# Neighbourhood scores: the low part of the queries in a zero-padded tile per head

## The chip, the cores and the metric

The kernel runs on one core of a Trainium2 chip. The metric is the time of one execution on the device in microseconds, lower is better. Engines are named as in the profile: PE is TensorE (PEld its weight load), DVE is VectorE, ACT is ScalarE, POOL is GpSimd, SP issues the DMAs.

## The reference

Two layers of a mixer work on 1024 latent tokens (a grid of 16 rows by 64 columns) and, as a prefix, 256 context tokens, 1024 features wide. In each layer one projection of the modulated input feeds three head groups: a gated convolution, a bidirectional retention (6 heads of 64) and a neighbourhood attention (6 heads of 64). The change is in the attention alone:

```python
s_loc = einsum('bhcd,bhrckd->bhcrk', q_r, k_win) * scale + bias   # window of 8 rows x 16 columns
s_ctx = einsum('bhcd,bhjd->bhcj', q_r, k_ctx) * scale             # all 256 context keys
p = softmax(concatenate([s_loc, s_ctx]))
o = p_loc @ v_win + p_ctx @ v_ctx
```

In the first layer the context tokens too are queries, over the context keys alone; the second layer needs no outputs for them.

## The kernel before

Everything is float32 in value. Matmuls whose result must be exact to float32 take their operands in two parts, a high one rounded to the matmul's fast format (`R`, float32r) and a low one that holds the rest (`x - high`). A product of two such operands is summed in three passes: high by high, low by high, high by low. Projections (`accumulate`, tile ps_pj) do so with three matmuls per 128 rows of contraction, over 512 or 256 columns.

For the scores a head has only 64 features, so two passes are packed into one matmul of 128 rows. For a pair of heads p, the key tile `KS[128, 2, TOK]` has for head hh the high part of its keys in rows 64*hh to 64*hh+63 and the low part in the other 64 rows. The query tile `QH[128, 2, TOK]` has the high part of the queries in both halves. `QH` by `KS` over 128 rows is thus high by high plus high by low. The missing low by high is a second matmul into the same bank, with `QL[128, TOK]`, which holds the low part of head 0's queries in rows 0 to 63 and of head 1's in rows 64 to 127. That matmul takes 64 rows: those of the head.

`natten_conv` runs once per layer. Keys and queries of a pair of heads are projected (`keys`, `queries`, with the evacuations `k_evac` and `q_evac`), then `core` runs as a side stream: it works through items, one step each, while the projections of the convolution, the gates and the next pair run between them. A latent item is a tile of 128 queries of one head (`s_lat`): scores over the 256 context keys (bank sc) and over a window of 384 keys, or 256 at the grid's two edges (bank sl), both from the ring ps_s of two banks; then on DVE the bias is added and the maximum taken (L746, L749, L751), ACT takes the exponential (L753), and DVE normalizes (L693, L694), all in the tile `P`. Two steps later (LAG = 2) `turn` transposes P on PE into ps_pt, and ACT and DVE copy it to `PT`. Two steps after that, for every second item, `pv` multiplies with the values of both heads (ps_pv). In a step the order on PE is: scores, then pv, then the transposes. A context item (`s_ctx`, layer 0 only, four per pair) has one score product over 256 keys.

The bias tables `B` (L713, L718) are built by POOL at the start of each pair. POOL also takes every fourth of the weight splits (L217) and some gate products (L364).

What sets the order: the program of PE stands in the order in which the code issues it. `Order` keeps a planned time `t`, to which every matmul adds its `cost`, and continues a side stream when its planned time has come. The other engines take their instructions in the order of the code's dependencies, and a tile ring (`bufs`) makes a writer wait for the buffer's last reader. `mm` is at L85 and `transpose` at L126, so all matmuls carry these two lines; they are told apart by tile names.

Of the kernel before, what the change touches and what calls it, by code (L numbers as in the profile page):

```python
# [30 lines left out]
LAG = 2  # L31
# [4 lines left out]


class Order:
    """Interleaves the matmul streams: the running one and those that wait for other engines."""

    def __init__(self):
        self.t = 0.0
# [36 lines left out]
def backbone(ctx: ExitStack, tc: tile.TileContext, io):  # L79
# [47 lines left out]
        od.t += 109  # L127
        od.poll()

    # ------------------------------------------------------- modulation tables  # L130
    class Mod:
        def __init__(self, l):
            self.l = l
# [2 lines left out]
            self.tab = const.tile([128, 24, 2], F, tag="mods", bufs=2, name="mods")  # L136

        def load(self, alloc, c0, w):
            """Two tiles [128, 4, w] of w_mod's columns c0:c0+w."""
            out = []  # L140
            for hf in range(2):
                t = alloc()
                sp.dma_start(t, io["w_mod"][self.l, hf * 512:(hf + 1) * 512, c0:c0 + w]
                             .rearrange("(k p) c -> p k c", p=128))
                out.append(t)
            return out
# [4 lines left out]
                   hf == 0, hf == 1, 80 * w // 128)  # L151

        def columns(self, ps, bank, parts):
            """Sums of the four row groups of ps, turned into columns of the table."""
            n = sum(k for _, k, _ in parts)
            m2 = const.tile([128, 512], F, tag="m2", name="m2")
            act.copy(m2[:, :n * 128], ps)
            yield 800
            pt = bank()
            for s in range(n):  # L160
                transpose(pt[:, s * 128:(s + 1) * 128], m2[:, s * 128:(s + 1) * 128])
            for o, k, blk in parts:
                t = const.tile([128, 4, 2], F, tag="msum", bufs=2, name="msum")
                dve.tensor_reduce(
                    t[:, :k], pt[:, o * 128:(o + k) * 128].rearrange(
                        "p (s g v) -> p s v g", g=4, v=32)[:, :, 0:2], AX.X, ALU.add)
                self.add_bias(t[:, :k], k, blk)
# [5 lines left out]
                ALU.add, ALU.add)  # L173

        def background(self, blocks, tmp):
            """The table's columns of some pairs of blocks, off the tensor engine."""
            def load(blk, kk):
                t = tmp.tile([128, 256], F, tag="wm", bufs=4, name="wm")
                sp.dma_start(t, io["w_mod"][self.l, kk * 128:(kk + 1) * 128,
                                            blk * 128:blk * 128 + 256])  # L180
                return t

            todo = [(blk, kk) for blk in blocks for kk in range(KC)]
            tiles = [load(*x) for x in todo[:2]]
            yield 2500
            for i, (blk, kk) in enumerate(todo):
                if i + 2 < len(todo):
                    tiles.append(load(*todo[i + 2]))
                t = tiles.pop(0)
                if kk == 0:  # L190
                    acc = const.tile([128, 2, 256], F, tag="m2", name="acc")
                for v in range(2):
                    c = cs[:, kk, v:v + 1]
                    if kk == 0:
                        dve.tensor_scalar(acc[:, v], t, c, None, ALU.mult)
                    else:
                        dve.scalar_tensor_tensor(acc[:, v], t, c, acc[:, v], ALU.mult, ALU.add)  # L197
                yield 2100
                if kk == KC - 1:
                    yield 1000  # L200
                    pt = ps_t()
                    for j in range(2):
                        for v in range(2):
                            o = (2 * j + v) * 128
                            transpose(pt[:, o:o + 128], acc[:, v, j * 128:(j + 1) * 128])
                    m = const.tile([128, 2, 2], F, tag="msum", bufs=2, name="msum")
                    dve.tensor_reduce(m, pt.rearrange("p (s v i) -> p s v i", s=2, v=2),
                                      AX.X, ALU.add)
                    self.add_bias(m, 2, blk)

    # ---------------------------------------------------------------- weights
    flip = [0]

    def split_lo(lo, raw, hi):
# [34 lines left out]
            t.append(split(raw, "w"))  # L249
        return lambda kk, i: t[kk // 2][i][:, (kk % 2) * 256:(kk % 2 + 1) * 256]  # L250

    # ------------------------------------------------------------------ input
    def new_h():
        return [[hpool.tile([128, KC, n], R, tag=f"h{j}{g}", name=f"h{j}{g}")
                 for j in range(2)] + [[]] for g, (o, n) in enumerate(GRP)]
# [24 lines left out]
                evac(g, ps[:, :GRP[g][1]], GRP[g][1])  # L280

    def h_tile(h, mods, t, xz, tmp):
        """Transposed, modulated and split columns of a token tile, as a side stream."""
        g = 2 if t >= 8 else t // 4
        off = t * 128 - GRP[g][0]
        v = 1 if g == 2 else 0
# [14 lines left out]
            pool.tensor_tensor(lo, ht, f32(hi), ALU.subtract)  # L301
            yield 1000

    # ---------------------------------------------------------------- decays
    def decay_tables(l, tmp):
        x = tmp.tile([128, 12], F, tag="dk", bufs=8, name="dk")
        sp.dma_start(x, io["decay"][l:l + 1, :].to_broadcast([128, 12]))
# [57 lines left out]
            sp.dma_start(yT[y_block * 128:(y_block + 1) * 128, o:o + n], y[:, :n])  # L365
        return f

    # ------------------------------------------------------------- retention
    def rope_evac(t2, rc, rs, dst, scale):
        def f(g, ps, n):  # L370
            o = GRP[g][0]
# [11 lines left out]
    def retention(l, h, yT, vn, ctx_q, begin):  # L383
        groups = (0, 1, 2)
        qgroups = groups if ctx_q else (0, 1)
        with ExitStack() as st:
# [33 lines left out]
            def core(p, kT, qT, V, oT):  # L420
# [29 lines left out]
                               kfb[:, hh].rearrange("p f d -> p (f d)"), True, True, 141)  # L450

                def chains():
                    """States before each chunk, transposed, in both directions."""
                    seqs = ([8, 9, 0, 1, 2, 3, 4, 5, 6, 7], [9, 8, 7, 6, 5, 4, 3, 2, 1, 0])
                    for fb in range(2):
                        dve.memset(ST[:, seqs[fb][0], fb], 0.0)
                    for i in range(9):
                        for fb in range(2):
                            a, b = seqs[fb][i:i + 2]
                            dve.scalar_tensor_tensor(  # L460
                                ST[:, b, fb], ST[:, a, fb], dec["gc"][:, fb, p:p + 1],
                                U(a)[:, fb * HD:(fb + 1) * HD], ALU.mult, ALU.add)
# [157 lines left out]
                proj_T(l, C_RG + 128 * p, gate_evac(t2, normed, Y_RET[p], yT),  # L620
                       h, (2, 0, 1) if ctx_q else (0, 1))

    # ------------------------------------------- neighbourhood and convolution
    def natten_conv(l, h, yT, vn, ctx_q, aside, w_out):
        qgroups = (2, 0, 1) if ctx_q else (0, 1)
        groups = (0, 1, 2) if ctx_q else (0, 1)
# [1 line left out]
        with ExitStack() as st:  # L628
# [3 lines left out]
            np_ = np_cm.__enter__()  # L632

            def flipped(t, o, rows):
                """Rows, blocks and columns of four tiles of reversed queries."""
                return bass.AP(tensor=t.tensor, offset=t[:, o:o + 1].offset,
                               ap=[list(t.ap[0]), [-8, rows], [8 * rows, 4], [-1, 8]])

# [19 lines left out]
            def q_evac(QH, QL):  # L658
                def f(g, ps, n):
# [14 lines left out]
                    for hh in range(2):  # L674
                        a, b = 64 * hh, 64 - 64 * hh
                        dve.tensor_copy(sel(QH[a:a + 64, hh]), src[a:a + 64])
                        act.copy(sel(QH[b:b + 64, hh]), src[a:a + 64])
                        dve.tensor_tensor(sel(QL[a:a + 64]), src[a:a + 64],
                                          f32(sel(QH[a:a + 64, hh])), ALU.subtract)
                return f  # L680

            def scores(dst, QH, QL, KS, hh, qo, ko, n):
                a = 64 * hh
                mm(dst, QH[:, hh, qo:qo + 128], KS[:, hh, ko:ko + n], True, False, n / 2.35)
                mm(dst, QL[a:a + 64, qo:qo + 128], KS[a:a + 64, hh, ko:ko + n], False, True,
                   n / 2.35)

            def col(nm):
                return np_.tile([128, 1], F, tag=nm, bufs=3, name=nm)
# [4 lines left out]
                dve.tensor_scalar(P[:, :n], P[:, :n], r, 0.5, ALU.mult, ALU.mult)  # L694

            def window(k):
                """First tile and number of tiles of the keys near a block of eight columns."""
                return max(k - 1, 0), 3 if 0 < k < 7 else 2

            def core(p, QH, QL, KS, oN):  # L700
# [22 lines left out]
                def s_ctx(i):  # L723
# [3 lines left out]
                    nm = col("nm")  # L727
                    dve.tensor_reduce(nm, sc[:, :256], AX.X, ALU.max)
                    dve.tensor_scalar(nm, nm, -1.0, None, ALU.mult)
                    P = np_.tile([128, 640], F, tag="P", bufs=LAG + 2, name="P")  # L730
                    s1 = col("sa")
                    act.activation(P[:, :256], sc[:, :256], AF.Exp, bias=nm, accum_out=s1)
                    normalize(P, 256, s1)
# [2 lines left out]
                def s_lat(i):  # L736
# [5 lines left out]
                    scores(sc[:, :256], QH, QL, KS, hh, k * 128, SEQ, 256)  # L742
                    scores(sl[:, :n], QH, QL, KS, hh, k * 128, k0 * 128, n)
                    m0, mx, nm = col("m0"), col("mx"), col("nm")
                    P = np_.tile([128, 640], F, tag="P", bufs=LAG + 2, name="P")
                    dve.tensor_tensor_reduce(  # L746
                        P[:, :256], sc[:, :256], zero.to_broadcast([128, 256]), 1.0, LOW,
                        ALU.add, ALU.max, m0)
# [6 lines left out]
                    return P  # L755

                def turn(P, nt):
                    PT = np_.tile([128, 640], F, tag="PT", bufs=4, name="PT")
                    pt = ps_t()
                    for i in range(min(nt, 4)):  # L760
                        transpose(pt[:, i * 128:(i + 1) * 128], P[:, i * 128:(i + 1) * 128])
# [94 lines left out]
                    yield from conv(b)  # L856

            cu = conv_units()
            KSs = [np_.tile([128, 2, TOK], R, tag="KS", name="KS") for _ in range(3)]
            state = {}  # L860

# [2 lines left out]

            def queries(p):
                QH = np_.tile([128, 2, TOK], R, tag="QH", bufs=1, name="QH")
                QL = np_.tile([128, TOK], R, tag="QL", bufs=1, name="QL")
                proj_T(l, C_NQ + 128 * p, q_evac(QH, QL), h, qgroups)
                return QH, QL

# [37 lines left out]
            next(cu)  # L908
            od.finish(job)

    # -------------------------------------------------------------- layers
    mod = Mod(0)
    h = new_h()
    x1 = dram.tile([SEQ, DM], F, name="x1")
# [18 lines left out]
    have = set()  # L933

    def stage(kks, tiles):
        """Modulation columns of some feature blocks, and those blocks transposed and split."""
        nk = len(kks)
        yield 0 if kks[0] == 0 else 2500
        ps = ps_v()
# [69 lines left out]
        q_ev(2, ps[:, :CTX], CTX)  # L1009

    def early(l, h):
        """The next layer's first products, held in PSUM while the last rows are normalized."""
        wk, wq = w_cols(l, C_RK), w_cols(l, C_RQ)
        todo = [(wk, 0, pj()), (wq, 0, pj()), (wk, 1, pj()), (wq, 1, ps_s())]
        for w, g, ps in todo:
# [10 lines left out]
    for l in range(DEPTH):  # L1026
# [12 lines left out]
        with ExitStack() as st:  # L1039
            wo, held, op, job = [], [], None, None  # L1040

            def gate_rows(v, held):
                """The gate of one modulation on all partitions, left in two banks."""
                for hf in range(2):
                    ps = ps_s()
                    dg = const.tile([128, 512], F, tag="m2", name="dg")
# [196 lines left out]
```

## Time and profile before

| | |
|---|---|
| time, median of 3 runs | 1476.04 us (1475.06 to 1476.51) |
| span of the profiled execution | 1474.9 us |
| PE busy | 1435.3 us, 97% of the span |
| PEld, DVE, ACT, POOL busy | 1168.4, 964.6, 469.0, 324.9 us |
| DMA | 126.32 MB, mean 86 GB/s |

The page gives the profiled execution by its span, 1474.9 us from the first to the last instruction; no time of its own around it is listed, so the span is what a sum can be made against, 1.1 us below the median of the runs. Of a group's row, the form "64*128 64x256" reads: the weights have 64 rows and 128 columns, 256 columns are streamed over 64 rows. "mean ns of one" of a matmul includes the depth of the array and overlaps the next one; the distance between two starts is what a matmul takes from PE.

### The profile page before, as it was taken

The page shows a single profiled execution, that of the slowest core. Times are in us where ns is not written, and L with a number is a line of the kernel's source. Part 1 is how long each engine was busy: PE and PEld are TensorE (multiplying, and loading weights), DVE is VectorE, ACT ScalarE, POOL GpSimd, SP SyncE. Part 2 cuts the span into 40 slices and gives each one's busy share as a digit, 9 for nine tenths or more (in the row PEclk, how much of TensorE's full clock was granted, in tenths as well). Part 3 has the DMA queues.
Part 4 walks back from the last instruction along what each step waited for, and adds up shares of the span by engine and source line. Part 5 has one row for each costly group of instructions (what it writes and reads, how often), then busy time and mean ns, then how long its engine had stood idle before and what let it go on. Part 6 is the DMA issues. An engine that isn't in the chain of part 4 may idle for free.

```text
span 1474.9 us, 23843 instructions
## 1 busy us (share of the span) xinstructions
PE 1435.3 (97%) x9016; PEld 1168.4 (79%) x9016; DVE 964.6 (65%) x2392; ACT 469.0 (32%) x985; POOL 324.9 (22%) x277
## 2 busy tenths in 40 slices
PE   7999999999999999999999999999999999999997
PEld 4787888787788778778887898888777877877886
DVE  4766474557767776765787656566487645355586
ACT  3322121223442443334344322122233434344310
POOL 1405041332003103000344405141320031110021
PEclk9999999999999999999999999999999999999999
DMA  9611101133123223116443211111241210301642
GB/s 289 198 55 29 48 16 47 58 113 91 40 79 107 73 60 116 44 33 193 162 142 108 78 47 30 48 34 57 93 118 51 61 58 29 89 22 52 213 158 86
DMA packets 160851, 126.32 MB, mean 86 GB/s; under 512 B 10320, under 2 KB 146144, under 8 KB 160736
## 3 DMA queue, kind: packets, MB, share of 16 engines
q1 hardware_dynamic: 160736, 124.80, 27.9%
q8 instruction: 71, 1.16, 0.3%
q14 instruction: 44, 0.36, 0.1%
HBM read 103.01 MB, written 21.76 MB: 85 GB/s over the span
## 4 chain that ended last, share of the span: by engine, by line
PE 86%; DVE 7%; DMA 3%; POOL 1%; issue 1%; SPq 1%; ACT 1%; POOLq 0%; DVEq 0%; ACTq 0%
PE ps_pj L85 63%; PE ps_s L85 9%; PE ps_pt L126 7%; PE ps_pv L85 6%; DMA wm<-in_w_mod 1%; DVE acc L197 1%; DVE rsw L379 1%; PE ps_pt L85 1%; POOL B L713 1%; DMA E<-in_rpb 1%; DMA wr<-in_w_in 0%; DMA x<-in_x 0%; DVE ret_q L508 0%; DVE qd L487 0%; DVE ret_s L499 0%
## 5 line engine op out<-in xcount | busy, mean ns | idle before, releaser
L85 PE MATMUL ps_pj<-h,wh 128*128 128x512 f32 (+1 forms) x2128 | 622.2, 373 | 3.2 <-ACT wh L225 3.2
L85 PEld LDWEIGHTS ps_pj<-h,wh 128*128 128x128 f32 x2128 | 378.4, 189 | 68.0 <-issue 5.5
L85 PE MATMUL ps_pj<-h,wl 128*128 128x512 f32 (+1 forms) x1064 | 396.4, 373 | 0.0
L85 PEld LDWEIGHTS ps_pj<-h,wl 128*128 128x128 f32 x1064 | 201.0, 189 | 33.7 <-issue 4.0
L85 PE MATMUL ps_pj<-wh,h 128*128 128x256 f32 x960 | 183.0, 291 | 0.0
L85 PE MATMUL ps_pj<-wo,yh 128*128 128x512 f32 (+1 forms) x608 | 182.0, 381 | 0.0
L85 PEld LDWEIGHTS ps_pj<-wh,h 128*128 128x128 f32 x960 | 156.1, 199 | 1.9 <-issue 1.8
L217 POOL TENSOR_TENSOR wl<-wr,wh 128x512 fp32r<-128x512 f32 x32 | 43.4, 1358 | 510.1 <-ACT wh L225 426.2
L85 PE MATMUL ps_pj<-wl,h 128*128 128x256 f32 x480 | 139.8, 291 | 5.0 <-DVE wl L217 2.9
L85 PEld LDWEIGHTS ps_pj<-wo,yh 128*128 128x128 f32 x608 | 112.0, 188 | 21.2 <-issue 0.5
L85 PE MATMUL ps_pj<-wo,yl 128*128 128x512 f32 (+1 forms) x304 | 116.2, 382 | 0.0
L225 ACT CAST wh<-wr 128x512 fp32r<-128x512 f32 x128 | 79.3, 621 | 115.2 <-PE ps_pj L85 103.8
L197 DVE SCALAR_TENSOR_TENSOR acc<-wm,c_silu,acc 128x256 f32<-128x256 f32 x224 | 109.5, 530 | 4.9 <-DMA wm<-in_w_mod 4.5
L763 ACT COPY PT<-ps_pt 128x512 f32<-128x512 f32 (+1 forms) x108 | 60.6, 561 | 149.3 <-PE ps_pt L126 149.1
L753 ACT ACTIVATE P<-P,nm 128x640 f32<-128x640 f32 (+1 forms) x96 | 77.2, 804 | 77.7 <-DVE nm L751 72.8
L85 PEld LDWEIGHTS ps_pj<-wl,h 128*128 128x128 f32 x480 | 95.5, 199 | 5.8 <-DVE wl L217 3.1
L217 DVE TENSOR_TENSOR wl<-wr,wh 128x512 fp32r<-128x512 f32 x96 | 68.8, 720 | 32.2 <-ACT wh L225 30.6
L85 PE MATMUL ps_s<-KS,QL 64*128 64x256 f32 x204 | 81.8, 401 | 0.0
L126 PE MATMUL ps_pt<-c_ident,P 128*128 128x128 f32 x480 | 75.8, 285 | 1.4 <-DVE P L694 1.3
L85 PE MATMUL ps_s<-KS,QH 128*128 128x256 f32 x204 | 71.3, 350 | 2.9 <-DVE mx L749 2.8
L85 PEld LDWEIGHTS ps_s<-KS,QL 64*128 64x128 f32 x204 | 37.3, 183 | 40.5 <-issue 34.4
L126 PEld LDWEIGHTS ps_pt<-c_ident,P 128*128 128x128 f32 x480 | 50.8, 140 | 19.3 <-issue 12.3
(174 smaller groups left out, 1970.5 us busy)
## 6 DMA issues: line engine op xcount, KB each, us to landing
wr<-in_w_in SPq DMA_DIRECT2D x104, 256.0 KB
wm<-in_w_mod SPq DMA_DIRECT2D x128, 128.0 KB
wr<-yT SPq DMA_DIRECT2D x36, 256.0 KB
yT<-ystage SPq DMA_DIRECT2D x32, 256.0 KB
wr<-in_w_out SPq DMA_DIRECT2D x32, 256.0 KB
wm<-in_w_mod SPq DMA_DIRECT2D x12, 512.0 KB
wr<-in_w_in SPq DMA_DIRECT2D x48, 128.0 KB
z<-in_x SPq DMA_DIRECT2D x8, 512.0 KB
```

What stands on the lines that cost most here:

```text
L85: pe.matmul(out, lhsT, rhs, start=start, stop=stop)
L126: pe.transpose(out, in_, ident[:in_.shape[0], :in_.shape[0]])
L197: dve.scalar_tensor_tensor(acc[:, v], t, c, acc[:, v], ALU.mult, ALU.add)
L217: eng.tensor_tensor(lo, raw, f32(hi), ALU.subtract)
L225: act.copy(hi, raw)
L379: dve.tensor_tensor(sw, sw, rs[:, o:o + n], ALU.mult)
L713: pool.tensor_tensor(B, bass.AP(tensor=E.tensor, offset=E[:, o:o + 1].offset, ap=[list(E.ap[0]), [1, nc_], [RPB_W, 16]]), rmask.unsqueeze( ...
L753: act.activation(P[:, :256 + n], P[:, :256 + n], AF.Exp, bias=nm, accum_out=s)
L763: act.copy(PT[:, :n], pt[:, :n])
```

## The change

`QL` becomes a tile `[128, 2, TOK]`, with a plane for each head as in `QH`: head hh's low part in rows 64*hh to 64*hh+63 of plane hh, zeros in the other 64 rows. It is allocated once per layer; the zeros are written once, by two memsets on POOL, and the queries of all three pairs go to the same other rows. The second matmul of `scores` then runs over 128 rows with all of `KS`'s plane; the zeros meet the low part of the keys and add nothing. The planned cost of a score matmul is `n / 2.2` instead of `n / 2.35`. QL takes 5 KB more per partition; the rings of `P` and `PT` have one buffer fewer each (three instead of four), which is 5 KB less.

```diff
@@ q_evac
-                        dve.tensor_tensor(sel(QL[a:a + 64]), src[a:a + 64],
+                        dve.tensor_tensor(sel(QL[a:a + 64, hh]), src[a:a + 64],
                                           f32(sel(QH[a:a + 64, hh])), ALU.subtract)
...
             def scores(dst, QH, QL, KS, hh, qo, ko, n):
-                a = 64 * hh
-                mm(dst, QH[:, hh, qo:qo + 128], KS[:, hh, ko:ko + n], True, False, n / 2.35)
-                mm(dst, QL[a:a + 64, qo:qo + 128], KS[a:a + 64, hh, ko:ko + n], False, True,
-                   n / 2.35)
+                for i, Q in enumerate((QH, QL)):
+                    mm(dst, Q[:, hh, qo:qo + 128], KS[:, hh, ko:ko + n], i == 0, i == 1, n / 2.2)
...
@@ s_ctx and s_lat
-                    P = np_.tile([128, 640], F, tag="P", bufs=LAG + 2, name="P")
+                    P = np_.tile([128, 640], F, tag="P", bufs=LAG + 1, name="P")
...
@@ turn
-                    PT = np_.tile([128, 640], F, tag="PT", bufs=4, name="PT")
+                    PT = np_.tile([128, 640], F, tag="PT", bufs=3, name="PT")
...
             cu = conv_units()
+            QL = np_.tile([128, 2, TOK], R, tag="QL", bufs=1, name="QL")
+            for hh in range(2):
+                pool.memset(f32(QL[64 - 64 * hh:128 - 64 * hh, hh]), 0.0)
             KSs = [np_.tile([128, 2, TOK], R, tag="KS", name="KS") for _ in range(3)]
...
@@ queries
-                QL = np_.tile([128, TOK], R, tag="QL", bufs=1, name="QL")
```

The order on PE, DVE, ACT and SP is the same row for row, although the planned costs differ. On PE, at an item of the grid's edge in layer 0, both programs have these rows (the shape is that of the output; h by wh and wl is a projection, KS by QH and QL the scores, PT by VA the value products, c_ident by P the transposes of an earlier item):

```order
L85 MATMUL ps_pj<-h_93,wh 128x256
L85 MATMUL ps_s<-KS,QH 128x256
L85 MATMUL ps_s<-KS,QL 128x256
L85 MATMUL ps_s<-KS,QH 128x256
L85 MATMUL ps_s<-KS,QL 128x256
L85 MATMUL ps_pv<-PT,VA 64x128 x10
L126 MATMUL ps_pt<-c_ident,P 128x128 x5
L85 MATMUL ps_pj<-h_94,wh 128x256
```

Nothing moved there; the two rows with QL have 128 rows of weights now instead of 64.

On POOL, where the neighbourhood part of layer 0 begins (ystage by oT is the last gate product of retention, wl a weight split, B a bias table), before:

```order
L550 TENSOR_TENSOR r_3392<-c_3390,mhalf 128x8
L364 TENSOR_TENSOR ystage<-tanh,oT 128x512
L217 TENSOR_TENSOR wl<-wr,wh 128x512
L713 TENSOR_TENSOR B<-E,c_rmask 128x256
L713 TENSOR_TENSOR B<-E,c_rmask 128x384
```

and with the change:

```order
L550 TENSOR_TENSOR r_3392<-c_3390,mhalf 128x8
L364 TENSOR_TENSOR ystage<-tanh,oT 128x512
L859 MEMSET QL 64x1280 x2
L217 TENSOR_TENSOR wl<-wr,wh 128x512
L711 TENSOR_TENSOR B<-E,c_rmask 128x256
L711 TENSOR_TENSOR B<-E,c_rmask 128x384
```

The two memsets stand between retention's last gate product and the next weight split; in layer 1 they stand at the same place.

More of the change, by code (lines that the diff above doesn't have):

```diff
@@ L744, in s_lat @@
                     m0, mx, nm = col("m0"), col("mx"), col("nm")
-                    P = np_.tile([128, 640], F, tag="P", bufs=LAG + 2, name="P")
+                    P = np_.tile([128, 640], F, tag="P", bufs=LAG + 1, name="P")
                     dve.tensor_tensor_reduce(
```

## The prediction

> **What bounds the kernel now.** I read the page first: busy shares, clock, and the chain that ended last.
>
> ```profile
> span 1474.9 us, 23843 instructions
> PE 1435.3 (97%) x9016; PEld 1168.4 (79%) x9016; DVE 964.6 (65%) x2392; ACT 469.0 (32%) x985; POOL 324.9 (22%) x277
> PEclk9999999999999999999999999999999999999999
> PE 86%; DVE 7%; DMA 3%; POOL 1%; issue 1%; SPq 1%; ACT 1%; POOLq 0%; DVEq 0%; ACTq 0%
> PE ps_pj L85 63%; PE ps_s L85 9%; PE ps_pt L126 7%; PE ps_pv L85 6%; DMA wm<-in_w_mod 1%; DVE acc L197 1%; DVE rsw L379 1%; PE ps_pt L85 1%; POOL B L713 1%; DMA E<-in_rpb 1%; DMA wr<-in_w_in 0%; DMA x<-in_x 0%; DVE ret_q L508 0%; DVE qd L487 0%; DVE ret_s L499 0%
> ```
>
> TensorE (PE) is the bound: 86% of the chain, at full clock. The score matmuls, which write ps_s, are on it with 9%, though part of those are retention's. So what a score matmul takes from PE counts almost one for one, as long as VectorE (DVE) keeps up. Next the groups of the score matmuls, shapes apart, and for contrast a group that has 128 rows and 256 columns everywhere.
>
> ```profile
> L85 PE MATMUL ps_s<-KS,QL 64*128 64x256 f32 x132 | 50.3, 381 | 0.0
> L85 PE MATMUL ps_s<-KS,QH 128*128 128x384 f32 x72 | 31.8, 441 | 2.6 <-DVE mx L749 2.6
> L85 PE MATMUL ps_s<-KS,QL 64*128 64x384 f32 x72 | 31.5, 438 | 0.0
> L85 PEld LDWEIGHTS ps_s<-KS,QL 64*128 64x128 f32 x204 | 37.3, 183 | 40.5 <-issue 34.4
> L85 PEld LDWEIGHTS ps_pj<-wh,h 128*128 128x128 f32 x960 | 156.1, 199 | 1.9 <-issue 1.8
> ```
>
> The low matmuls are 132 of 256 columns and 72 of 384, and as many high ones. Their means of 381 and 438 ns include the pipeline's depth and are no price. The last two rows are the lead: 204 loads of 64-row weights left the load path idle for 34.4 us with nothing that it waited for, 960 loads of 128-row weights for 1.8 us. The price itself is the distance from one matmul's start to the next one's, which the timeline of PE shows (first column the start, second the duration).
>
> ```profile
> 410.72 0.39 PE L85 MATMUL ps_pj<-h,wl 128*128 128x512 f32 x1
> 410.95 0.28 PE L85 MATMUL ps_s<-KS,QH 128*128 128x256 f32 x1
> 411.15 0.38 PE L85 MATMUL ps_s<-KS,QL 64*128 64x256 f32 x1
> 411.46 0.44 PE L85 MATMUL ps_s<-KS,QH 128*128 128x384 f32 x1
> 411.83 0.44 PE L85 MATMUL ps_s<-KS,QL 64*128 64x384 f32 x1
> 412.20 0.77 PE L126 MATMUL ps_pt<-c_ident,P 128*128 128x128 f32 x5
> 412.72 0.71 PE L85 MATMUL ps_pj<-h,wh 128*128 128x512 f32 x2
> ...
> 419.33 0.40 PE L85 MATMUL ps_pj<-h,wh 128*128 128x256 f32 x2
> 419.57 0.28 PE L85 MATMUL ps_pj<-h,wl 128*128 128x256 f32 x1
> 419.69 0.40 PE L85 MATMUL ps_pj<-h,wh 128*128 128x256 f32 x2
> 419.93 0.28 PE L85 MATMUL ps_s<-KS,QH 128*128 128x256 f32 x1
> 420.13 0.38 PE L85 MATMUL ps_s<-KS,QL 64*128 64x256 f32 x1
> ```
>
> In a stream that stays on 128 rows, a 256-column matmul takes 0.12 us (419.33 to 419.57 is two, 419.57 to 419.69 one), a 512-column one 0.23 (410.72 to 410.95). In the scores, the rows alternate 128, 64, 128, 64 and the distances are 0.20, 0.31, 0.37 and 0.37: 1.25 us for one item of 256 + 384 columns. Every boundary between a 128-row and a 64-row matmul costs about 0.09 to 0.2 us beyond the columns.
>
> **The change, part by part.**
>
> *The padded low matmul.* All four matmuls become 128*128. For 384 columns no undisturbed row exists; halfway between 0.12 at 256 and 0.23 at 512 lies 0.175. What follows the last low matmul is read from the code: of 108 items (six head pairs of 16 latent items, four context items more in each pair of layer 0), 42 are followed by the value products (ps_pv), 54 by transposes (ps_pt), 12 by a projection; 33 of the 42 and 39 of the others end on 384 columns, the rest on 256. For those two I need the same successor after an all-128-row matmul:
>
> ```profile
> 337.69 0.39 PE L85 MATMUL ps_pj<-h,wh 128*128 128x512 f32 x1
> 337.92 0.60 PE L126 MATMUL ps_pt<-c_ident,acc 128*128 128x128 f32 x4
> 338.28 0.48 PE L85 MATMUL ps_pj<-h,wl 128*128 128x512 f32 x1
> ...
> 650.93 0.40 PE L85 MATMUL ps_pj<-h,wh 128*128 128x512 f32 x1
> 651.25 1.31 PE L85 MATMUL ps_pv<-PT,VA 128*64 128x128 f32 x20
> ```
>
> Into transposes nothing is lost (0.23, as within the stream), and four of them take 0.36, so five 0.47, where after a 64-row matmul they took 0.52: 0.05 more to win. Into ps_pv, whose form is 128*64, 0.32 instead of 0.23: a switch of 0.09 remains. The sum by boundary:
> - high 256 to low 256, 0.20 to 0.12: 132 x 0.08 = 10.6 us
> - low 256 to the next high, 0.31 to 0.12: 96 x 0.19 = 18.2
> - high 384 to low 384, 0.37 to 0.175: 72 x 0.195 = 14.0
> - low 384 to transposes, 0.195 + 0.05: 39 x 0.245 = 9.6
> - low 384 to ps_pv, 0.37 to 0.265: 33 x 0.105 = 3.5
> - last low 256 to transposes or a projection, 0.19 + 0.05: 27 x 0.24 = 6.5
> - last low 256 to ps_pv, 0.31 to 0.21: 9 x 0.10 = 0.9
>
> Together 63.3 us off PE, about 11 in each head pair of layer 0 and 10 in each of layer 1.
>
> *What of it VectorE gives back.* A shorter PE needs the same VectorE work in less time. Windows around the first five head pairs, and one slice:
>
> ```profile
> core 0: us, PE busy (x) PEld busy (x) DVE busy (x) ACT busy (x) POOL busy (x), PEclk, DMA share, GB/s
> 345.00:420.00 75.00, 73.68 (x442) 56.14 (x440) 60.09 (x187) 29.78 (x66) 10.17 (x9) 1.00 0.22 63
> 460.00:535.00 75.00, 75.00 (x450) 57.16 (x448) 57.00 (x184) 29.17 (x64) 13.70 (x14) 1.00 0.27 81
> 575.00:648.00 73.00, 72.71 (x450) 54.45 (x449) 55.27 (x189) 27.08 (x61) 10.83 (x10) 1.00 0.17 51
> 1085.00:1157.00 72.00, 70.47 (x408) 52.37 (x407) 58.58 (x177) 28.78 (x59) 9.76 (x9) 1.00 0.23 65
> 1187.00:1255.00 68.00, 67.75 (x394) 50.18 (x393) 38.15 (x132) 27.08 (x55) 12.55 (x12) 1.00 0.13 40
> ...
> 1080.00:1100.00 20.00, 18.47 (x82) 14.04 (x81) 19.01 (x44) 7.40 (x17) 8.48 (x8) 1.00 0.38 107
> ```
>
> In the first pair of layer 0, 60.1 us of VectorE work would sit in 75 - 11 = 64 us, 94%; in the first of layer 1, 58.6 in 62, 95%; in layer 0's other two about 90%; in the second of layer 1, 38.2 in 58, 66%. VectorE can be filled to 95% (19.01 of 20 us in the slice), but there PE already waits for it:
>
> ```profile
> PE ps_s L85 <- DVE mx L749: 2.8, 5, 1.5
> PE ps_pt L126 <- DVE P L694: 1.3, 1, 1.3
> ```
>
> Only 4.1 us in six waits, so elsewhere PE has slack. Where it waits, at the start of a head pair, a faster PE wins nothing: there the bias tables are being built (POOL B L713 is on the chain with 1%) and VectorE is full. I take the first two or three items of four head pairs as lost (about 2.5 x 0.6 x 4 = 6) and 1 us for full stretches later: 7 us back. Bounds: 0 if the slack covers all; 21 if VectorE could not go over 85% in the four pairs that it fills (layer 0's three, and layer 1's first: 60.1 / 0.85 = 70.7 of 75 us, so the two fullest would win only about 4 us instead of 11, the other two about 8).
>
> *The zeroing.* Two memsets of 64x1280 per layer on GpSimd (POOL), ahead of the first split there:
>
> ```profile
> 316.70 1.29 POOL L364 TENSOR_TENSOR ystage<-tanh,oT 128x512 f32<-128x512 f32 x1 [4.23 <-DVE oT L569]
> 328.46 1.36 POOL L217 TENSOR_TENSOR wl<-wr,wh 128x512 fp32r<-128x512 f32 x1 [10.47 <-ACT wh L225]
> ...
> 1073.52 1.29 POOL L217 TENSOR_TENSOR wl<-wr,wh 128x512 fp32r<-128x512 f32 x1 [10.10 <-ACT wh L225]
> ```
>
> No memset of that size is in the trace. At the rate of the subtraction (1.36 us for 512 columns) 1280 columns take 3.4 us, two 6.8, inside the 10.47 and 10.10 us for which POOL sits idle just there. If that cover were gone, the split behind them, and with it one projection, would be a few us late, twice. I take 0; 6 at worst.
>
> *Shorter rings.* P and PT go from 4 buffers to 3. Item s writes P after its scores; the buffer's last reader is the transposition of item s-3, which PE does one step earlier, ahead of those scores. PT's last reader is the value product that PE issues just ahead of the transposes which fill it anew. Both waits are over when the awaited scores and transposes are, so 0. *Evacuation:* the same instructions, another address, 0. The planner's cost of a score matmul rises by 6%, but PE's order stays the same row for row.
>
> Sum: 63 - 7 = 56 us off the profiled span of 1474.9, 1419. That span is 1.1 us under the median of the runs, so against the median 1476.0 - 56 = **1420 us**.
>
> **Rivals.**
> 1. *VectorE becomes the bound* of the four full head pairs. For it: the two windows at 94 and 95%. Against: waits of PE are few today, and much of VectorE's idle time is its own wait for scores. By the 85% bound, 63 - 21 = 42 off: 1434.
> 2. *The weight load stays exposed, so nothing is won.* The distances 0.31 and 0.37 are also 0.12 and 0.175 plus one load of 0.19, so the load, not the row count, might be what each low matmul waits for. Against it: the 960 all-128-row loads, as long (199 ns) and hidden. If it held for the scores, the distances 0.31 and 0.37 would stay and the first boundary of each item would rise from 0.20 to at most 0.31, 132 x 0.11 = 15 us: 1476 to 1491.
>    The Trainium skill, "TensorE: Matmul & The Clock Gate", Part 3, The mechanism, states that weight loads overlap running matmuls only where their row groups differ; by it the padded form, with one row group for all, would gain nothing, and the stream at 419.33 contradicts it.
> 3. *Slower: the three-buffer rings make a chain.* If the release of P came later than I read it, each item would wait for the transposition of the one before. It decides from 56 / 108 = 0.52 us per item on; a wait of 1 us in each, twice that, gives 1476 - 56 + 108 = 1528. Against it: PE's order above.
>
> **How the numbers follow.** Forecast 0.73 (1409 to 1427), rival 1 0.20 (1427 to 1440), rival 2 0.03, rival 3 0.04. The forecast's lower end is the full 63 us and 4 for what the second decimal of the starts leaves open; the range reaches up to rival 1's 1434: 1409 to 1434. What a measurement can tell from no change is about 0.2%, 3 us. Faster 0.93 (forecast and rival 1), same 0.02 and slower 0.05 (rival 2 split between them, and rival 3).
>
> **What would show it.** Right: in the timeline after, high and low scores 0.12 and 0.17 us apart, the load's idle "issue" time gone, both QL groups 128*128 with the durations of QH in a stream, VectorE's share up from 65% to 68% with the same busy time. More waits of PE for "DVE mx L749" and "DVE P L694", some 5 to 10 us, at the starts of head pairs: my 7. Wrong: distances still of 0.3 us (rival 2), such waits over 20 us (rival 1), or the waits of ScalarE or VectorE for PE on P and PT at every item (rival 3).

## The result and the profile after

The changed kernel takes 1421.48 us (median of 4 runs, 1415.35 to 1424.96) against 1476.28 us before; the ratio is 0.9623, 95% interval [0.9597, 0.9648]. A second series on another occasion gave 1421.70 us and 0.9614 [0.9601, 0.9627]. The forecast was 1420 us.

From the page after: the span, the busy times and the chain by line.

```profile
span 1420.3 us, 23906 instructions
PE 1371.0 (97%) x9016; PEld 1156.0 (81%) x9016; DVE 959.7 (68%) x2392; ACT 469.0 (33%) x985; POOL 330.1 (23%) x281
PE ps_pj L85 62%; PE ps_pv L85 6%; PE ps_pt L126 6%; PE ps_s L85 6%; DVE acc L197 1%; DVE rsw L379 1%; DMA E<-in_rpb 1%; PE ps_pt L85 1%; POOL B L711 1%; DVE P L692 1%; DVE ret_q L508 0%; DVE qd L487 0%; DVE wl L217 0%; DVE ret_s L499 0%; DVE sm L406 0%
```

PE is as full as before (97%), over a span shorter by 54.6 us. VectorE did the same work in it, 68% instead of 65%. The scores' part of the chain went from 9% to 6%. Now the low matmuls and their weight load, shapes apart:

```profile
L85 PE MATMUL ps_s<-KS,QL 128*128 128x256 f32 x132 | 36.6, 283 | 0.0
L85 PE MATMUL ps_s<-KS,QL 128*128 128x384 f32 x72 | 24.3, 338 | 0.0
L85 PEld LDWEIGHTS ps_s<-KS,QL 128*128 128x128 f32 x204 | 38.9, 191 | 3.7
```

The load takes about as long as before (191 ns, 183 then), but its path sits idle for 3.7 us in all instead of 40.5. The timeline of PE at a latent item shows what became of the distances:

```profile
396.17 0.39 PE L85 MATMUL ps_pj<-h,wl 128*128 128x512 f32 x1
396.40 0.28 PE L85 MATMUL ps_s<-KS,QH 128*128 128x256 f32 x1
396.51 0.28 PE L85 MATMUL ps_s<-KS,QL 128*128 128x256 f32 x1
396.63 0.34 PE L85 MATMUL ps_s<-KS,QH 128*128 128x384 f32 x1
396.81 0.34 PE L85 MATMUL ps_s<-KS,QL 128*128 128x384 f32 x1
396.98 0.71 PE L126 MATMUL ps_pt<-c_ident,P 128*128 128x128 f32 x5
397.45 0.71 PE L85 MATMUL ps_pj<-h,wh 128*128 128x512 f32 x2
```

0.11, 0.12, 0.18 and 0.17 us, 0.58 per item instead of 1.25, and the five transposes behind take 0.47 instead of 0.52. The weight loads of three of these matmuls show how the time was lost, before and then with the change (timeline of PEld; the matmuls' starts are in the prediction and above):

```profile
411.15 0.18 PEld L85 LDWEIGHTS ps_s<-KS,QL 64*128 64x128 f32 x1 [0.24 <-issue]
411.46 0.19 PEld L85 LDWEIGHTS ps_s<-KS,QH 128*128 128x128 f32 x1
411.83 0.18 PEld L85 LDWEIGHTS ps_s<-KS,QL 64*128 64x128 f32 x1 [0.18 <-issue]
```

```profile
396.40 0.19 PEld L85 LDWEIGHTS ps_s<-KS,QL 128*128 128x128 f32 x1
396.52 0.19 PEld L85 LDWEIGHTS ps_s<-KS,QH 128*128 128x128 f32 x1
396.63 0.19 PEld L85 LDWEIGHTS ps_s<-KS,QL 128*128 128x128 f32 x1
```

Before, each load begins together with its own matmul (411.15, 411.46 and 411.83). That holds wherever the row form changes: at all 204 low matmuls the load begins 1 to 3 ns ahead of its matmul. With the change it begins one matmul earlier (396.40 for the matmul at 396.51), 0.12 us ahead in the median, and is hidden behind that one.

What PE waits for, in the list of its waits (total us, times, longest):

```profile
PE ps_s L85 <- DVE mx L747: 7.6, 9, 1.8
PE ps_pt L126 <- DVE P L692: 2.9, 1, 2.9
PE ps_s L85 <- DVE m L744: 1.5, 2, 0.8
```

These were 2.8 and 1.3 us before, the third absent: 7.9 us more. One more loss is behind the second row. The timeline of PE at the first context items of layer 0, and the windows after it and after the waits at 1061 to 1067 us (columns: stretch, its length, busy us of PE, PEld, DVE, ACT, POOL, granted clock, DMA share, GB/s):

```profile
350.64 0.28 PE L85 MATMUL ps_s<-KS,QL 128*128 128x256 f32 x1
353.80 0.44 PE L126 MATMUL ps_pt<-c_ident,P 128*128 128x128 f32 x2 [2.87 <-DVE P L692]
...
356.70 0.63 PE L85 MATMUL ps_pj<-h,wl 128*128 128x512 f32 x1
357.12 0.41 PE L85 MATMUL ps_s<-KS,QH 128*128 128x256 f32 x1
```

```profile
355.00:360.00 5.00, 5.00 (x20) 4.19 (x19) 3.25 (x12) 2.46 (x9) 1.88 (x2) 0.66 0.21 60
1065.00:1070.00 5.00, 3.18 (x14) 2.51 (x15) 4.93 (x13) 1.80 (x4) 3.72 (x5) 0.84 0.18 54
1070.00:1075.00 5.00, 5.00 (x24) 4.18 (x23) 3.01 (x12) 2.51 (x6) 0.95 (x1) 0.82 0.35 105
```

After PE had waited for 2.9 us, its clock was granted at 0.66 over the next slice: a 512-column matmul takes 0.42 us there (356.70 to 357.12) instead of 0.23. Over these slices the clock cost 5 x (0.34 + 0.16 + 0.18) = 3.4 us. Before the change the slice from 355 to 360 us and the four from 1088 to 1108 us were all at 1.00. The loss does not follow every such wait: in the profiled execution of the second series PE waited 0.7, 1.8 and 0.5 us between 1064 and 1073 us, and the slices from 1065 to 1075 us were at 1.00.

### The profile page after: what moved, and what is told of

Same layout as the page of the kernel before. It is cut to its first block, busy times and chain, and to the rows that moved or that the text cites. A ratio compares the mean times of both kernels' runs of the same rounds, so it can differ in the third digit from the quotient of the medians.

```text
span 1420.3 us, 23906 instructions
## 1 busy us (share of the span) xinstructions
PE 1371.0 (97%) x9016; PEld 1156.0 (81%) x9016; DVE 959.7 (68%) x2392; ACT 469.0 (33%) x985; POOL 330.1 (23%) x281
## 4 chain that ended last, share of the span: by engine, by line
PE 80%; DVE 9%; issue 2%; DMA 1%; POOL 1%; ACT 1%; SPq 0%; POOLq 0%; DVEq 0%; ACTq 0%
PE ps_pj L85 62%; PE ps_pv L85 6%; PE ps_pt L126 6%; PE ps_s L85 6%; DVE acc L197 1%; DVE rsw L379 1%; DMA E<-in_rpb 1%; PE ps_pt L85 1%; POOL B L711 1%; DVE P L692 1%; DVE ret_q L508 0%; DVE qd L487 0%; DVE wl L217 0%; DVE ret_s L499 0%; DVE sm L406 0%
## 5 line engine op out<-in xcount | busy, mean ns | idle before, releaser
L85 PE MATMUL ps_s<-KS,QH 128*128 128x256 f32 x204 | 59.7, 311 | 9.3 <-DVE mx L747 7.6
L85 PEld LDWEIGHTS ps_pj<-wo,yl 128*128 128x128 f32 x304 | 57.2, 188 | 10.8 <-issue 0.5
L126 PEld LDWEIGHTS ps_pt<-c_ident,P 128*128 128x128 f32 x480 | 54.5, 141 | 13.9 <-issue 7.4
L85 PE MATMUL ps_pv<-PT,VA 128*64 128x128 f32 x960 | 64.3, 278 | 0.0
```

Source lines behind the costliest of these rows:

```text
L85: pe.matmul(out, lhsT, rhs, start=start, stop=stop)
L126: pe.transpose(out, in_, ident[:in_.shape[0], :in_.shape[0]])
```

## The experiments

All times stand beside runs of the kernel before on the same chip.

**Everything but the padded matmul.** The changed kernel, with the low matmul on 64 rows again:

```diff
-                for i, Q in enumerate((QH, QL)):
-                    mm(dst, Q[:, hh, qo:qo + 128], KS[:, hh, ko:ko + n], i == 0, i == 1, n / 2.2)
+                a = 64 * hh
+                mm(dst, QH[:, hh, qo:qo + 128], KS[:, hh, ko:ko + n], True, False, n / 2.2)
+                mm(dst, QL[a:a + 64, hh, qo:qo + 128], KS[a:a + 64, hh, ko:ko + n], False, True,
+                   n / 2.2)
```

> The changed kernel with one part undone: the low matmul of the scores again takes only the 64 rows of its head, out of the new two-plane tile; the zeroing, the rings of three, the planned cost of n/2.2 and the addresses stay. Theory (the whole gain comes from the boundaries between 64-row and 128-row matmuls): the distances are 0.20, 0.31, 0.37, 0.37 us again and the time is that of the kernel before, 1476 us, within 3. Rival (the shorter rings or the other addresses cost or win something that the 56 us hide): 1480 us or more, with ScalarE or VectorE waiting for PE on P or PT, or 1470 or less.

1477.43 us against 1477.58, ratio 1.0001 [0.9992, 1.0011]. The low matmuls are back to

```profile
L85 PE MATMUL ps_s<-KS,QL 64*128 64x256 f32 x132 | 50.3, 381 | 0.0
```

word for word the row of the kernel before. The rings of three, the zeroing, the addresses and the planned cost together are worth nothing that can be measured; the whole gain is the matmul's.

**Two switches per item.** The kernel before, unpadded, with the matmuls of a latent item grouped by their rows:

```diff
-                    scores(sc[:, :256], QH, QL, KS, hh, k * 128, SEQ, 256)
-                    scores(sl[:, :n], QH, QL, KS, hh, k * 128, k0 * 128, n)
+                    a, qo = 64 * hh, k * 128
+                    parts = ((sc, SEQ, 256), (sl, k0 * 128, n))
+                    for dst, ko, w in parts:
+                        mm(dst[:, :w], QH[:, hh, qo:qo + 128], KS[:, hh, ko:ko + w], True, False,
+                           w / 2.35)
+                    for dst, ko, w in parts:
+                        mm(dst[:, :w], QL[a:a + 64, qo:qo + 128], KS[a:a + 64, hh, ko:ko + w],
+                           False, True, w / 2.35)
```

> The kernel before, with unpadded 64-row low matmuls, but in each latent item both high matmuls are issued first and then both low ones, so that an item changes between 128 and 64 rows twice instead of four times. Theory A (each change of the row form costs, and inside a run of equal form the weight load hides): distances 0.12, 0.265, 0.12 and 0.37 us, 0.875 instead of 1.25, over 96 items 36 us of PE time off; with some 4 us given back to VectorE about 1444 us. Rival B (a 64-row weight load never hides, whatever stands before it): the second low matmul starts 0.31 after the first, 1.065 per item, 18 us off, about 1459 us. Rival C (64-row matmuls are slow by themselves, whatever their order): no gain, 1476 us.

1447.05 us, ratio 0.9789 [0.9776, 0.9802]: 30.5 us off with not one row padded. The timeline of PE (both high matmuls in one row, then both low ones):

```profile
399.79 0.45 PE L85 MATMUL ps_s<-KS,QH 128*128 128x256 f32 x2
400.18 0.56 PE L85 MATMUL ps_s<-KS,QL 64*128 64x256 f32 x2
400.67 0.77 PE L126 MATMUL ps_pt<-c_ident,P 128*128 128x128 f32 x5
```

0.39 and 0.49, 0.88 us per item, as theory A had it in sum; B's 1.065 and C's 1.25 are out. A's parts are not right, though. The medians of the four distances over all items with a window of 384 are 0.114, 0.270, 0.223 and 0.265 us. The second low matmul does not start 0.12 behind the first but 0.22, 0.10 over the first one's columns, and the way back costs 0.09, not 0.19. The loads show what happens. At the two changes they again begin only with their matmul (median 2 ns ahead of it). The second low load begins 0.107 us after the start of the first low matmul, and its own matmul follows 0.116 later, as far behind its load as in a stream of one form. So a change of the row form costs twice: about 0.09 ahead of the matmul that changes, and up to 0.10 more behind it, where its load began no earlier than itself. Two changes in immediate succession pay both at the second, 0.19. What holds the load back at a change stays open.

**The background sums later.** The changed kernel; only the start of VectorE's background sums is moved:

```diff
-        def background(self, blocks, tmp):
+        def background(self, blocks, tmp, lead=0):
...
+            if lead:
+                yield lead
             tiles = [load(*x) for x in todo[:2]]
...
-            yield from mod_l.background(range(16, 24, 2), tmp)
+            yield from mod_l.background(range(16, 24, 2), tmp, 45000)
```

> The changed kernel, but the background sums of the modulation columns on VectorE (acc, line 197) start 45 us of planned time later in each layer, so that the first head pair's start has VectorE for itself; all else is the same work. Theory D (the gain that was missing against the 63 us sum is lost at the start of the first head pairs, where VectorE is full with the background sums while GpSimd builds the bias tables): the waits of 2.9 us at 351 us and of about 4 us at 1061 to 1067 us go, and with them the two slices in which the TensorE clock is granted at 0.66 to 0.84 right after; 5 to 9 us less than the changed kernel's 1421 us, about 1414 us. Rival (the tables alone set those waits): no change, 1421 us within 3. The background work could also collide with the later head pairs, whose VectorE share is already 85%: then 1421 us or more with new waits at 400 to 610 us.

1436.93 us, ratio 0.9728 [0.9714, 0.9741], 15 us slower than the changed kernel. The waits at 351 and 1061 us went, as theory D said; but others took their place at the next pairs (2.6 us at 456, 1.8 and 2.7 at 562 and 566, 0.7 and 1.8 at 1162 us), and in layer 0 the sums no longer end before the neighbourhood part does. The timeline of PE there:

```profile
662.11 0.28 PE L85 MATMUL ps_pj<-h,wl 128*128 128x256 f32 x1
665.21 0.85 PE L126 MATMUL ps_pt<-c_ident,acc 128*128 128x128 f32 x4 [2.82 <-DVE acc L199]
668.05 2.08 PE L85 MATMUL ps_s<-dg,c_ones 128*128 128x512 f32 x2 [2.00 <-DVE dg L1049]
```

PE stands for the last sums and for the gate rows that need them, and from 670 to 680 us its clock is granted at 0.50. By the starts of the same matmuls, PE loses 13 us on the changed kernel's between 649 and 702 us. The work was hidden where it stood; a start 45 us later puts its end outside the cover.

**The bias tables earlier.** In the changed kernel `core`'s loads of E and its building of B became functions, called earlier:

```diff
             keys(0)
-            job = begin(0, queries(0))
+            bias = tables(raw_bias(0))
+            job = begin(0, queries(0), bias)
...
                 Q = queries(p)
+                bias = tables(raw_bias(p))
                 proj_T(l, *gate(p - 1), h, groups)
-                job = begin(p, Q)
+                job = begin(p, Q, bias)
```

> The changed kernel, but the loads of the relative position bias and the building of the bias tables on GpSimd are issued earlier: for the first head pair ahead of its queries' projection, for the others between the queries' projection and the gate of the pair before, instead of when the item stream starts. Theory E (the waits of PE for the score maximum, DVE mx, at the starts of the pairs come from the tables being late): the waits of 0.8 to 2 us at 1061 to 1067, 1153 to 1157 and 1241 to 1246 us go, about 8 us with layer 1 alone, and the one at 351 us too, since GpSimd no longer works beside VectorE there: 1409 to 1413 us. Rival (VectorE's own load sets them): the waits stay and the time is 1418 to 1424 us. A third way: GpSimd, which takes its work in order, waits for the bias loads ahead of a weight split and makes a projection late; then the same or slower, with PE waiting for POOL wl.

1422.96 us, ratio 0.9633 [0.962, 0.9646], no gain in sum. In layer 1 the theory held: the waits at the pairs' starts went, and the n-th matmul of PE, 11.3 us behind the changed kernel's at the layer's start, was 4.7 behind at its end, 6.6 us won. In layer 0 it lost more than that at the second and third pair: two waits of 3.2 and 3.7 us at 459 and 566 us, with the clock at 0.50 behind the second (570 to 575 us), put PE 4.3 and 6.2 us further behind. From the list of PE's waits, and POOL's and VectorE's timelines at the second pair:

```profile
PE ps_s L85 <- ACT P L738: 6.9, 2, 3.7
```

```profile
442.74 2.90 POOL L715 TENSOR_TENSOR B<-E,c_rmask 128x256 f32<-128x256 f32 x3 [25.55 <-DMA E<-in_rpb]
```

```profile
452.66 4.53 DVE L197 SCALAR_TENSOR_TENSOR acc<-wm,c_silu,acc 128x256 f32<-128x256 f32 x6
...
460.51 0.41 DVE L734 TENSOR_REDUCE nm<-ps_s 128x1 f32<-128x256 f32 x1
```

ScalarE's exponential waits for the maximum of the context item (nm), and that stands on VectorE behind a burst of background sums. None of the three theories named this.

**The changed kernel again, and the tables earlier only where it helped.** The second is the kernel above with one condition, so that only the first pair of each layer and layer 1's other pairs build early:

```diff
-                bias = tables(raw_bias(p))
+                bias = None if ctx_q else tables(raw_bias(p))
...
+                if bias is None:
+                    bias = tables(raw_bias(p))
```

> The changed kernel as it is, for a ratio beside the next two. 1421 us; its runs so far lay between 1415.4 and 1425.0 and the span falls as the granted clock rises (1423.1 us at 0.990, 1413.6 at 0.998), so a spread of some 8 us again, more than the kernel before shows.

> The changed kernel with the bias tables built earlier only where that helped: for the first head pair of both layers and for the other two of layer 1, not for the other two of layer 0. Theory (in layer 1 the late tables set the waits of PE, in layer 0's second and third pair the background sums on VectorE do): layer 1 wins the 6.6 us by which the row of PE in its trace caught up there, the first pair of layer 0 some 0.6: 1414 us, and no wait of PE for the maximum, DVE mx, at the starts of layer 1's pairs. Rival (the wins in layer 1 were only the earlier losses of layer 0 caught up): 1421 us.

The changed kernel: 1421.70 us (1419.01 to 1422.23, 0.9614), no wider than the kernel before in the same series (1474.08 to 1478.70); the larger spread that was expected is not there. The other: 1412.20 us, ratio 0.9560 [0.9547, 0.9573], 9.5 us under the changed kernel and the best of all. Its waits for the maximum, and the window over the first pair of layer 1 beside the same window of the changed kernel (the second row):

```profile
PE ps_s L85 <- DVE mx L757: 1.3, 4, 0.4
```

```profile
1045.00:1110.00 65.00, 62.96 (x395) 51.96 (x394) 57.49 (x174) 29.86 (x62) 4.58 (x4) 1.00 0.24 72
```

```profile
1045.00:1110.00 65.00, 61.84 (x368) 51.21 (x369) 57.07 (x164) 28.07 (x57) 9.73 (x9) 0.97 0.28 80
```

7.6 us of waiting became 1.3, and in this window the clock stays at 1.00. The early tables bring waits of their own, 2.3 us at 330 us for VectorE's evacuation of the keys (KS) and 1.7 at 1057 us for that of the queries (QH, QL). Matmul by matmul its PE gains 6.8 us on the changed kernel's profiled execution of this series in layer 1 and 0.8 in layer 0. The other 2.1 us lie ahead of the attention, where the two kernels are the same: there the clock of the changed kernel's execution is at 0.70 from 70 to 75 us and at 0.81 and 0.85 from 145 to 155 us, and the other's is at 1.00. So in these two executions 7.6 us are the tables' work.

**The background later in layer 1 too.** The same, with the lead of 45 us in layer 1 alone:

```diff
-            yield from mod_l.background(range(16, 24, 2), tmp)
+            yield from mod_l.background(range(16, 24, 2), tmp, 45000 if mod_n is None else 0)
```

> As the one before, and in layer 1 alone the background sums on VectorE start 45 us of planned time later. In layer 1 there is a third as many of them as in layer 0, so the tail does not reach the end of the part. Theory (VectorE, full with background sums, makes the first queries' split late, 1.2 + 1.0 us in the trace with early tables): those two waits go, 1412 us. Rival (the sums collide with the second pair instead, as they did with late tables, 0.9 + 2.0 us): 1414 to 1416 us.

1419.12 us, ratio 0.9613 [0.9594, 0.9631], 7 us slower than without: the rival, and more than it said.

```profile
PE ps_s L85 <- DVE m L756: 4.5, 2, 3.8
```

The sums collide with the second pair: one wait of 3.8 us at 1149 us, and the clock at 0.85 and 0.81 over the two slices from 1150 to 1160 us. In layer 1's attention PE fell 4.9 us behind the kernel without the lead. Two trials to move VectorE's background failed in the same way.

**Without the background sums.** Both kernels with

```diff
-            yield from mod_l.background(range(16, 24, 2), tmp)
+            dve.memset(mod_l.tab[:, 16:24], 0.5)
             if mod_n is not None:
-                yield from mod_n.background(range(0, 16, 2), tmp)
+                dve.memset(mod_n.tab[:, 0:16], 0.5)
+            yield 2500
```

> The kernel before without the background sums: the modulation columns that the neighbourhood part computes beside its items are left out (their table is set to 0.5), with their loads, VectorE sums and transposes. A base for the next run. TensorE loses 12 blocks' transposes (48 of 0.11 us, some 5 us with the switch around them) and the one wait of 1.4 us at 352 us: about 1469 us.

> The changed kernel without the same background sums. The question is what became of the 7 us between the 63 us that the boundaries give and the 56 us measured. Theory (about half is VectorE's background, at 351 us and at 1061 to 1067 us, half the bias tables, at 1153 to 1157 and 1241 to 1246 us): this run is 59 to 61 us under the one before. Rival F (all of it is VectorE's background): 63 to 66 us under it. Rival G (all of it is the tables): 56 us under it.

1463.08 us and 1401.18 us (0.9905 [0.989, 0.992] and 0.9490 [0.9474, 0.9506]): 61.9 us apart, instead of about 55. The kernel before lost 14.5 us without the sums, twice what was expected; its trace has 64 of these transposes, not 48, and what else it lost stays open. So some 6 to 7 us of what the changed kernel gives back hang on the background sums. By PE's starts within the attention alone it is 9, 61.6 us apart without the sums and 52.6 with them, and 3.4 of these are the clock's, which stays at 1.00 in both attention parts without the sums. That is about half or more, less than all: between the theory's 59 to 61 and rival F's 63 to 66. What is left is in the waits, of the changed kernel and of the kernel before, both without the sums:

```profile
PE ps_s L85 <- DVE mx L747: 5.1, 6, 1.2
```

```profile
PE ps_s L85 <- DVE mx L749: 1.0, 2, 0.6
```

4.1 us more, all at the starts of layer 1's pairs, where the tables are late, but for one wait of 0.4: rival G's part, which building them earlier removed.

## Why the prediction was right

*The boundaries.* The mechanism and the size held: the changes of the row form are what the low matmuls cost, and the loads say in what way, since at a change they begin only with their matmul. With the medians of the starts before and after, the seven terms of the sum come to 65 us instead of 63.3. The first boundary went from 0.208 to 0.117 (12.0 us, 10.6 forecast). The projections behind the last low matmul were worth 0.30 instead of 0.24, because the first distance after a switch, 0.34 instead of 0.23, was not in the term. The value assumed for 384 columns, 0.175, measured 0.176, and the 0.265 to ps_pv 0.268. Grouping the rows without padding won about half, so the boundaries are the cause and not the zeros; undoing the padding alone took all of it away.

*What VectorE gives back* was the term mis-sized: 12.4 us, not 7. By the starts of the same matmuls before and after, PE was 0.9 us ahead when the attention of layer 0 began, 29.9 at its end, 31.0 when layer 1's began and 54.6 at its end, so the attention won 52.6 of the 65 (53.5 in the profiled execution of the second series, whose clock lost 1.7 less there). PE's additional waits are 7.9 of the 12.4. Another 3.4 are the clock, which the prediction did not have: it had priced a wait by its length alone. The last 1.1 is not assigned.

The place of the waits was half right. The term named layer 0's three pairs and layer 1's first, as those that fill VectorE. Two of them do have waits at their start, the first of each layer; layer 0's second and third have none there. About 3.5 of the 7.9 us came at layer 1's second and third pair instead. The second was one at 66% of VectorE in the prediction, and building the tables earlier removed these waits, so there the late tables set them and not a full VectorE.

That 1420 came out so near is in part luck. The 5.4 us more given back were offset by 1.7 more at the boundaries and by the 2.0 won outside the attention, which the change does not touch. There the two executions differ in the clock. Before the change it is at 0.66 from 70 to 75 us, where afterwards it is at 1.00, and where layer 1 begins it is lower for longer than in the slices from 810 to 820 us afterwards (0.74 and 0.92):

```profile
840.00:845.00 5.00, 2.65 (x12) 2.66 (x13) 3.92 (x9) 0.21 (x1) 1.67 (x2) 0.64 0.38 111
845.00:850.00 5.00, 5.00 (x32) 5.00 (x31) 3.90 (x23) 1.82 (x8) 0.00 (x0) 0.68 0.20 60
```

Up to PE's last matmul the slices under 1.00, worked out as above, cost 8.5 us in both executions; the clock's loss in the attention was made up elsewhere.

*The zeroing* was hidden. POOL's timeline:

```profile
317.18 2.38 POOL L859 MEMSET QL<- 64x1280 f32 x2
327.64 1.30 POOL L217 TENSOR_TENSOR wl<-wr,wh 128x512 fp32r<-128x512 f32 x1 [8.09 <-ACT wh L225]
```

The two memsets took 2.38 us, a third of the 6.8 assumed, and 8.09 of the 10.47 us of idle time are left. *The rings of three* cost nothing (the first experiment).

*The rivals.* VectorE as the bound of whole pairs did not come. The windows of a first pair of each layer after (stretch, length, busy us per engine, clock, DMA share, GB/s):

```profile
340.00:410.00 70.00, 67.13 (x449) 57.22 (x449) 62.96 (x193) 30.09 (x66) 10.03 (x9) 0.98 0.24 70
1054.00:1116.00 62.00, 58.84 (x374) 49.04 (x373) 54.00 (x167) 27.19 (x55) 9.73 (x9) 0.97 0.24 69
```

90% and 87% of VectorE over the pair, below the 94 and 95% that the rival took, with waits only at its start. The exposed load did not come either: an all-128-row stream hides a load of 191 ns behind matmuls 0.12 us apart, here in the scores as before in the projections. The rival was right on one thing, that the load was exposed before the change; but the change of the row form exposed it. The Trainium skill, "TensorE: Matmul & The Clock Gate", Part 3, The mechanism, lists that loads overlap running matmuls only if their row groups differ. By this line the load would have stayed exposed; the measurement decides against it, for here the loads overlapped where the rows were the same and not where they differed. The text above that line in the same section also names a background weight buffer, with which the overlap seen here would agree. The same page of the Trainium skill, Part 1, The two states you'll see, has a clock at half rate after an idle window of about 3.4 us. The trace agrees with the half rate (0.42 us for 512 columns), but a wait of 2.9 us was enough here.

## What to carry to other kernels

Price a matmul by the distance between starts, and look where the row form changes: a half-height matmul among full-height ones cost more than its zero-padded form, which was free here since the other operand already had all 128 rows. Where padding is not at hand, issue matmuls of one form together; that alone won 30 us. When PE gets faster, the next loss is where its work starts on tables and evacuations that are only just in time: make the late input earlier where that collides with nothing (in layer 0's second and third pair it lost time), and be slow to move hidden background work, for its end must stay under the cover too.

## What the runs showed of the hardware

- At a change between 64-row and 128-row matmuls the weight load began only with its own matmul (1 to 4 ns ahead of it), in a stream of one form 0.11 to 0.12 us ahead, with the matmul before. A change cost about 0.09 us of PE's time ahead of the matmul and up to 0.10 behind it; two in immediate succession cost 0.19 at the second.
- A wait of PE of 2.9 us was followed by matmuls at half rate, and a granted clock of 0.66 over 5 us, 1.7 us lost on top. Waits of 0.7, 1.8 and 0.5 us close together were followed by no such loss in one execution, waits of 0.6, 0.7 and 1.8 us by one of 1.7 us in another.
- VectorE's instructions were stretched while GpSimd built the bias tables, which adds to what VectorE has to do at the start of a pair. A background sum (acc) of the changed kernel took 0.43 us just before GpSimd began, and 1.1 to 1.2 us beside it (VectorE, then GpSimd):

```profile
346.66 1.28 DVE L197 SCALAR_TENSOR_TENSOR acc<-wm,c_silu,acc 128x256 f32<-128x256 f32 x3
348.19 1.11 DVE L197 SCALAR_TENSOR_TENSOR acc<-wm,c_silu,acc 128x256 f32<-128x256 f32 x1
```

```profile
348.14 3.24 POOL L711 TENSOR_TENSOR B<-E,c_rmask 128x256 f32<-128x256 f32 x3 [19.20 <-DMA E<-in_rpb]
```
